# A K=32 matmul padded to all 128 rows, and the filler matmuls of an attention loop gathered ahead of the readout

## The chip, the cores and the metric

The kernel runs on one core of one Trainium2 chip. The metric is device time in microseconds (us) of one execution; the median of three runs is compared. Engines are called PE (TensorE), DVE (VectorE), ACT (ScalarE) and POOL (GpSimd); PEld is PE's loading of weights, which the trace lists apart from the matmuls. "Weights" of a matmul is its stationary operand, whatever tensor that is.

## The reference, cut to what matters

A two-layer decoder trunk over 256 tokens of width 1024: a gated DeltaNet layer, then a sparse-attention layer with three branches (compressed, selection, window). The change lies in the second layer. With 256 tokens every selected block and the whole window are visible, so the selection and window branches are both causal attention over 256 keys; the compressed branch attends over 15 block summaries.

```
q = rope((x @ w_in)[:, :1024])                      # 16 heads of 64, 4 key groups
z = (x @ w_in)[:, 1024:4096]                        # 3 branches x 16 heads x 64
gates = sigmoid((x @ w_in)[:, 4096:])
k_cmp, v_cmp = compress_blocks(...)                 # 15 rows per key group
o_cmp = masked_softmax(q @ k_cmp.T) @ v_cmp
o_sel, o_win = causal softmax attention over k_sel/v_sel, k_win/v_win
o = sum over the 3 branches of gates * o_branch * silu(z_branch)
x = layer_norm(sqrt(2) * x + o @ w_out)
```

## The kernel before

All of the stage runs in one hand-written order: an engine executes its instructions in the order in which the Python code issues them. Tokens are two tiles of 128 rows (t = 0, 1). A **unit** is one or two heads of one tile: for t = 0 two heads (h, h+1), for t = 1 one head. The string UNITS sets the order of the 24 units: (0,0), (0,2), (1,0), (0,4), (1,1), (0,6), (1,2), ... "Round i" below is pass i of the main loop, which starts unit i and finishes unit i-1. For a unit:

- `scores` (L1327): four PE matmuls into a bank `s` (two such banks).
- `maxima` (L1336 to L1343): DVE adds the mask and takes row maxima.
- `exps` (L1356 to L1361): ACT writes exponentials `pt` and, for the compressed branch, `Pc`.
- `transposes` (L1369, L1371): PE turns `pt` into bank `ptp`, and Pc into 32 rows of the `s` bank: two heads x 16 compressed positions.
- `probs` (L1376, L1380): ACT copies them to `PT` and `PcT` (32 rows x 128).
- `readout` (L1395, L1398, L1401): PE multiplies PT with the values `vtok` (65 columns), and PcT with `vbd`, the compressed values of two heads laid out block-diagonally (32 rows x 130 columns), into the one bank `op`. An f32 matmul is two PE instructions. For t = 1 a readout needs two heads; where these are neighbours in the order, it is done in halves, and only the second half has L1401.
- `total` (L1409 to L1413): DVE divides, gates and sums `op` into `zz`, issued by `defer(1, ...)` at the next `step()`.

The other work of the loop is the projection z (`bz`): 48 **parts**, each two weight chunks of 128x512, six matmuls of 512 columns in bank `pbz` (`tm_part`, L233 to L235, a product split into three by high and low halves). `fill(n)` issues n parts. FA[i] and FB[i] say how many a round issues ahead of `exps` and behind the readout. Weights come by DMA into `raw_bz`, ACT casts the high half (`hi_bz`, L181), POOL subtracts for the low half (`lo_bz`, L185); eight pairs of buffers hold them, and `presplit` issues up to one chunk more a round. When a tile's four parts are done, ACT and DVE make z's gate of them (`th` L1227, `zz` L1228). From round 18 on `merges` is not empty and the parts are those of the output projection (`pbo`, `pbl`); t = 1 heads are merged by `tp_b` (L1427).

Of the kernel before, what the change touches and what calls it, by code (L numbers as in the profile page):

```python
# [9 lines left out]
F32 = mybir.dt.float32  # L10
# [7 lines left out]
P = 128  # L18
# [20 lines left out]
FA = "3113111011210212044211123"  # L39
FB = "0211121311122110212111000"  # L40

PRE, TAIL = 4, 2
NEG = -1e30

NSEL = 9
# [3 lines left out]
def make_consts():  # L49
# [8 lines left out]
    c = np.zeros((P, NCON_B), np.float32)  # L58
    cm = np.where(f <= p, np.float32(0), np.float32(NEG))
    n = np.arange(16)[None, :]  # L60
    for off, t in ((C_CM0, p), (C_CM1, p + P)):
        c[:, off:off + P] = cm
        c[:, off + P:off + 2 * P] = cm
        c[:, off + 256:off + 272] = np.where((n < 15) & (16 * n + 31 <= t), np.float32(0), np.float32(NEG))
    c[:, C_ROW:C_ROW + 1] = p >= 31
# [28 lines left out]
def trunk(ctx: ExitStack, tc: tile.TileContext, I: dict, out: bass.AP):  # L94
    nc = tc.nc
    V, S, G, PE = nc.vector, nc.scalar, nc.gpsimd, nc.tensor
# [7 lines left out]
    def defer(n, f):  # L104
        late.append([n, f])

    def step():
        for e in late:
            e[0] -= 1
        due = [e for e in late if e[0] <= 0]  # L110
        late[:] = [e for e in late if e[0] > 0]
        for _, f in due:
            f()
# [15 lines left out]
    wk = ph.enter_context(tc.tile_pool(name="wk", bufs=3))  # L129
# [35 lines left out]
    def split_to(n):  # L165
        while state["s"] < min(n, len(order)):
            lower()
            load_to(state["s"] + (NRAW))
            k = order[state["s"]]
            state["s"] += 1  # L170
            if k[0] == "w1":
                continue
            r = raws[k]
            h = ring.tile([P, 1024], F32R, tag="whi", name=f"hi_{k[0]}_{k[1]}", bufs=NSPL)
            l = ring.tile([P, 1024], F32R, tag="wlo", name=f"lo_{k[0]}_{k[1]}", bufs=NSPL)
            if k == order[1]:

                S.copy(h[:, 0:512], r[:, 0:512])
                V.tensor_copy(h[:, 512:1024], r[:, 512:1024])
            else:  # L180
                S.copy(h, r)  # L181
            e = V if state["s"] <= NVEC + 1 else G

            def f(l=l, r=r, h=h):
                e.tensor_tensor(l, r, h.bitcast(F32), op=ALU.subtract)  # L185

            if e is G:
                f()
            else:
                lows.append(f)  # L190
            splits[k] = (h, l)
# [4 lines left out]
    def lower():  # L196
        while lows:
            lows.pop(0)()
# [42 lines left out]
    def presplit():  # L241
        oldest = next(i for i, n in enumerate(uses) if n)
        split_to(min(state["top"] + PRE, oldest + NSPL, state["s"] + 1))
        lower()

    def fill(n, low=True):
        for _ in range(n):
            step()
            if fills:
                fills.pop(0)()  # L250
            if low:
                lower()
# [174 lines left out]
    def decay_diff(q):  # L427
# [6 lines left out]
        def causal(e):  # L434

            G.affine_select(e, e, pattern=[[0, 4], [1, P]], base=0, channel_multiplier=-1,
                            compare_op=ALU.is_ge, fill=NEG)

# [567 lines left out]
    def pool(name, bufs, **kw):  # L1006
        return ph.enter_context(tc.tile_pool(name=name, bufs=bufs, reuse_waits="tile", **kw))
# [5 lines left out]
    wk = pool("wkb", 2)  # L1013
# [8 lines left out]
    def tbank(name):  # L1022
        return pt_.tile([P, 512], F32, tag="t", name=name)
# [77 lines left out]
    G.memset(hpS, 0.0)  # L1101
    hid = wk.tile([P, 2, 4, 16], F32, name="hid", bufs=1)
    G.memset(hid, 0.0)
    vbd = wk.tile([32, 4, 2, 65], F32, name="vbd", bufs=1)
    bd = cb[0:32, C_BD:C_BD + 2]
    G.tensor_copy(vbd[:, :, :, 64], bd[:, None, :].to_broadcast([32, 4, 2]))
    fill(2)
    k_post()
    fill(4)
# [76 lines left out]
    def compressed_v():  # L1186

        vcp = tbank("vcp")
        for g_ in range(4):
            PE.matmul(vcp[0:32, g_ * 64:(g_ + 1) * 64], hr[:, g_].rearrange("p a b -> p (a b)"), w2[:, 256:320],  # L1190
                      start=True, stop=True)

        def place():
            for g_ in range(4):
                V.tensor_tensor(vbd[:, g_, :, 0:64], vcp[0:32, None, g_ * 64:(g_ + 1) * 64].to_broadcast([32, 2, 64]),
                                bd[:, :, None].to_broadcast([32, 2, 64]), op=ALU.mult)

        defer(1, place)
# [115 lines left out]
    units = [order0.pop(0) if k == "0" else order1.pop(0) for k in UNITS]  # L1314
    S_, PT_, PTT, PC, PCT, MX, TP = {}, {}, {}, {}, {}, {}, {}
    cnt = {"n": 0}

    def scores(u):
        t, h = u
        sp = S_[u] = sbank(f"s{t}{h}")  # L1320
        for j in range(2):
            hh = h + j if t == 0 else h
            lq = qT[hh // 8][:, hh % 8, t * P:(t + 1) * P]
            n = 272 if t == 0 or j == 0 else 256
            c0 = 272 if t == 1 and j == 1 else 0
            for i, kk in enumerate((kh, kl)):
                PE.matmul(sp[:, j, 0:n], lq, kk[:, hh // 4, c0:c0 + n], start=i == 0, stop=i == 1)  # L1327
# [17 lines left out]
    def exps(u):  # L1345
        t, h = u
        sp, mx = S_[u], MX[u]
        s4 = sp[:, :, 0:256].rearrange("p j (b k) -> p j b k", b=2)
        pt = PT_[u] = wk.tile([P, 2, 2, P], F32, tag="hl", name=f"pt{t}{h}", bufs=3)
        if t == 0 or h % 2 == 0:  # L1350
            PC[t, h] = wk.tile([P, 2, 16], F32, tag="Pc", name=f"Pc{t}{h}", bufs=4)
        Pc = PC[t, h - h % 2]
        if t == 0:
            for j in range(2):
                for b in range(2):
                    S.activation(pt[:, j, b, :], s4[:, j, b, :], AF.Exp, bias=mx[:, 2 * j + b:2 * j + b + 1])  # L1356
                S.activation(Pc[:, j, :], sp[:, j, 256:272], AF.Exp, bias=mx[:, 4 + j:5 + j])
        else:
            for b in range(2):
                S.activation(pt[:, :, b, :], s4[:, :, b, :], AF.Exp, bias=mx[:, b:b + 1])  # L1360
            S.activation(Pc[:, h % 2, :], sp[:, 0, 256:272], AF.Exp, bias=mx[:, 4:5])  # L1361

    def transposes(u):
        t, h = u
        pt = PT_[u]
        tp = TP[u] = tbank(f"ptp{t}{h}")
        for j in range(2):
            for b in range(2):
                PE.transpose(tp[:, (2 * j + b) * P:(2 * j + b + 1) * P], pt[:, j, b, :], ident)  # L1369
        if t == 0 or h % 2:  # L1370
            PE.transpose(S_[u][0:32, 1, 272:400], PC[t, h - h % 2 * t].rearrange("p a b -> p (a b)"), ident)  # L1371

    def probs(u):
        t, h = u
        PT = PTT[u] = wk.tile([P, 2, 2, P], F32, tag="ra", name=f"PT{t}{h}", bufs=6)
        S.copy(PT.rearrange("p a b c -> p (a b c)"), TP[u])  # L1376
        if t == 0 or h % 2:
            h -= h % 2 * t
            PCT[t, h] = wk.tile([32, P], F32, tag="PcT", name=f"PcT{t}{h}", bufs=2)
            S.copy(PCT[t, h], S_[u][0:32, 1, 272:400])  # L1380

    OP, summed = {}, set()

# [82 lines left out]
    merges, ready = [], []  # L1466
    cnt["t0"] = 0

    def advance():
        if merges:  # L1470
            merges.pop(0)()

    def merge0(q):
        merge(0, 4 * q, 4, tbank)
        if q:
            add_bo(0, [(c, part) for c in range(2) for part in range(4)])

    def merge1(g_):
        need_z(1, 3072)
        merge(1, 2 * g_, 2, tbank)  # L1480
        add_bo(1, [(0, g_)])
        if g_ == 3:
            add_bo(1, [(1, g_)])

    n = len(units)
    for i in range(n + 1):
        if i < n:
            scores(units[i])
        first = i < n and units[i][0] == 0 and not merges
        if first:  # L1490

            maxima(units[i])
        if i:
            probs(units[i - 1])
        step()
        if i < n and not first:
            maxima(units[i])
        fill(int(FA[i]))
        advance()
        presplit()  # L1500
        if i < n:
            exps(units[i])
        if i:
            t, h = units[i - 1]
            if t == 0:
                readout(t, h)
                if h == 14:
                    cnt["t0"] = 1
                    merges += [lambda: merge0(0), lambda: merge0(1)] + ready
            else:  # L1510

                if (units[i - 2] if h % 2 else units[i]) == (1, h ^ 1):
                    readout(t, h - h % 2, h % 2)
                elif h % 2:
                    readout(t, h - 1)
                if h % 4 == 3:
                    (merges if cnt["t0"] else ready).append(lambda g_=h // 4: merge1(g_))
        fill(int(FB[i]))
        if i < n:
            transposes(units[i])  # L1520
    while len(merges) > 1:
# [78 lines left out]
```

## Time and profile before

| | |
|---|---|
| median of 3 runs | 393.53 us (392.84 to 394.13) |
| the profiled execution | 393.95 us, its span 392.2 us |
| PE busy | 379.5 us of the span, 97% |
| DVE, ACT, POOL busy | 223.5, 220.4, 246.2 us |
| mean granted TensorE clock | 0.995 |

The busy time of PE overlaps itself (matmuls are pipelined and their ends are modelled), so the cost of PE work is read below from one start to the next start, not from durations.

### The profile page before, as it was taken

The numbers are of one execution on the slowest core, as the hardware profiler recorded it, in microseconds if no ns is written. First come the engines' busy times: TensorE is split into PE (matmuls) and PEld (weight loads), VectorE is DVE, ScalarE is ACT, GpSimd is POOL, SyncE is SP. The second block draws the span as 40 slices with busy tenths as digits, with TensorE's granted clock in tenths as the row PEclk, the third lists the DMA queues.
The fourth block names the chain that finished last, engine by engine and source line by source line (L and its number), as shares of the span: only waits on it lengthen the run. The fifth ranks groups of instructions, "written<-read, shape, count | busy, mean of one in ns | idle before, by whom it ended". The sixth has DMA issues, their size and how long they took to land.

```text
span 392.2 us, 7553 instructions
## 1 busy us (share of the span) xinstructions
PE 379.5 (97%) x2870; PEld 334.8 (85%) x2870; DVE 223.5 (57%) x591; ACT 220.4 (56%) x433; POOL 246.2 (63%) x154
## 2 busy tenths in 40 slices
PE   8999999999999999999999999999999999999991
PEld 6899999999979987877998788888888888878891
DVE  2868776678633455454541655645656465676726
ACT  4688766656654462625563649566474647456410
POOL 5699999747454846894754988193544637209051
PEclk9999999999999999999999999999999999999998
DMA  7876678754334315573636764343515243301011
GB/s 223 323 223 206 223 220 293 200 135 164 110 113 146 119 45 171 175 242 119 214 109 213 274 222 152 107 150 119 162 43 174 65 151 109 107 3 53 3 53 53
DMA packets 23476, 58.68 MB, mean 150 GB/s; under 512 B 6672, under 2 KB 9232, under 8 KB 23312
## 3 DMA queue, kind: packets, MB, share of 16 engines
q1 hardware_dynamic: 23232, 58.13, 44.7%
q8 instruction: 22, 0.36, 0.4%
q14 instruction: 14, 0.11, 0.1%
q10 hardware_dynamic: 144, 0.07, 0.1%
q0 software_dynamic: 64, 0.01, 0.0%
HBM read 55.96 MB, written 2.23 MB: 148 GB/s over the span
## 4 chain that ended last, share of the span: by engine, by line
PE 42%; DVE 4%; ACT 3%; DMA 2%; POOL 2%; issue 1%; POOLq 0%; DVEq 0%; SPq 0%; ACTq 0%
PE pbz L233 6%; PE pbz L234 6%; PE pbz L235 6%; PE op L1398 4%; PE s L1327 3%; PE ptp L1369 3%; DMA raw_bz<-in_bz 2%; PE op L1401 2%; PE op L1395 1%; ACT hi_bq L181 1%; POOL lo_bq L185 1%; PE pskv L235 1%; PE pbo L233 1%; PE pskv L233 1%; PE pskv L234 1%; PE qtp L1214 1%
## 5 line engine op out<-in xcount | busy, mean ns | idle before, releaser
L185 POOL TENSOR_TENSOR lo_bz<-raw_bz,hi_bz 128x1024 fp32r<-128x1024 f32 x24 | 56.8, 2390 | 39.1 <-ACT hi_bz L181 21.5
L185 POOL TENSOR_TENSOR lo_wqkv<-raw_wqkv,hi_wqkv 128x1024 fp32r<-128x1024 f32 x22 | 52.4, 2399 | 6.8 <-ACT hi_wqkv L181 4.7
L233 PE MATMUL pbz<-hi_bz,x1h 128*128 128x512 f32 x96 | 38.9, 405 | 0.0
L234 PE MATMUL pbz<-hi_bz,x1l 128*128 128x512 f32 x96 | 37.7, 393 | 0.0
L235 PE MATMUL pbz<-lo_bz,x1h 128*128 128x512 f32 x96 | 37.6, 392 | 0.0
L185 POOL TENSOR_TENSOR lo_bo<-raw_bo,hi_bo 128x1024 fp32r<-128x1024 f32 x8 | 18.8, 2384 | 22.8 <-ACT hi_bo L181 17.7
L185 POOL TENSOR_TENSOR lo_skv<-raw_skv,hi_skv 128x1024 fp32r<-128x1024 f32 x12 | 28.4, 2401 | 5.0 <-PE pskv L235 5.0
L185 POOL TENSOR_TENSOR lo_wz<-raw_wz,hi_wz 128x1024 fp32r<-128x1024 f32 x8 | 19.4, 2438 | 16.0 <-ACT hi_wz L181 15.9
L1376 ACT COPY PT<-ptp 128x512 f32<-128x512 f32 x24 | 14.1, 587 | 24.4 <-PE ptp L1369 24.4
L181 ACT CAST hi_bz<-raw_bz 128x1024 fp32r<-128x1024 f32 x24 | 25.3, 1053 | 2.9 <-DMA raw_bz<-in_bz 1.6
L185 POOL TENSOR_TENSOR lo_wo<-raw_wo,hi_wo 128x1024 fp32r<-128x1024 f32 x8 | 18.9, 2387 | 11.8 <-ACT hi_wo L181 11.8
L185 POOL TENSOR_TENSOR lo_bq<-raw_bq,hi_bq 128x1024 fp32r<-128x1024 f32 x8 | 19.1, 2394 | 11.6 <-ACT hi_bq L181 11.6
L181 ACT CAST hi_wqkv<-raw_wqkv 128x1024 fp32r<-128x1024 f32 x22 | 22.7, 1043 | 1.2 <-DMA raw_wqkv<-in_wqkv 1.2
L235 PEld LDWEIGHTS pbz<-lo_bz,x1h 128*128 128x128 f32 x96 | 18.0, 188 | 4.1
L233 PEld LDWEIGHTS pbz<-hi_bz,x1h 128*128 128x128 f32 x96 | 18.0, 188 | 4.1
L234 PEld LDWEIGHTS pbz<-hi_bz,x1l 128*128 128x128 f32 x96 | 18.0, 188 | 2.8
L1360 ACT ACTIVATE pt<-s,mx 128x256 f32<-128x256 f32 x32 | 13.4, 472 | 10.9 <-DVE mx L1343 8.7
L215 PE MATMUL pk<-xh,hi_wqkv 128*128 128x256 f32 x64 | 18.7, 292 | 0.0
L215 PE MATMUL pq<-xh,hi_wqkv 128*128 128x256 f32 x64 | 18.5, 289 | 0.0
L217 PE MATMUL pk<-xh,lo_wqkv 128*128 128x256 f32 x64 | 18.1, 283 | 0.0
L217 PE MATMUL pq<-xh,lo_wqkv 128*128 128x256 f32 x64 | 18.1, 283 | 0.0
L216 PE MATMUL pq<-xl,hi_wqkv 128*128 128x256 f32 x64 | 18.1, 283 | 0.0
(360 smaller groups left out, 1257.3 us busy)
## 6 DMA issues: line engine op xcount, KB each, us to landing
raw_bz<-in_bz SPq DMA_DIRECT2D x24, 512.0 KB, 3.3
raw_wqkv<-in_wqkv SPq DMA_DIRECT2D x23, 512.0 KB, 4.5
raw_skv<-in_skv SPq DMA_DIRECT2D x12, 512.0 KB, 3.3
raw_wz<-in_wz SPq DMA_DIRECT2D x8, 512.0 KB, 3.3
raw_wo<-in_wo SPq DMA_DIRECT2D x8, 512.0 KB, 3.4
raw_bq<-in_bq SPq DMA_DIRECT2D x8, 512.0 KB, 3.7
raw_bo<-in_bo SPq DMA_DIRECT2D x8, 512.0 KB, 3.3
raw_w<-in_w SPq DMA_DIRECT2D x4, 512.0 KB, 3.3
```

Source lines behind the costliest of these rows:

```text
L181: S.copy(h, r)
L185: e.tensor_tensor(l, r, h.bitcast(F32), op=ALU.subtract)
L215: PE.matmul(ps[:, 0:T], wh[:, kt, :], ah[:, kt, :], start=kt == 0, stop=False)
L216: PE.matmul(ps[:, 0:T], wh[:, kt, :], al_[:, kt, :], start=False, stop=False)
L217: PE.matmul(ps[:, 0:T], wl[:, kt, :], ah[:, kt, :], start=False, stop=kt == 7)
L233: PE.matmul(ps, ah[:, kt, tt], wh[:, k4, cols], start=kt == 0, stop=False)
L234: PE.matmul(ps, al_[:, kt, tt], wh[:, k4, cols], start=False, stop=False)
L235: PE.matmul(ps, ah[:, kt, tt], wl[:, k4, cols], start=False, stop=kt == 7)
L1327: PE.matmul(sp[:, j, 0:n], lq, kk[:, hh // 4, c0:c0 + n], start=i == 0, stop=i == 1)
L1360: S.activation(pt[:, :, b, :], s4[:, :, b, :], AF.Exp, bias=mx[:, b:b + 1])
L1376: S.copy(PT.rearrange("p a b c -> p (a b c)"), TP[u])
L1398: PE.matmul(o3[:, r, 1 + b, :], PT[:, j, b, :], vt_[:, b, j, g_, :], start=j == 0, stop=j == 1)
```

## The change

Two edits. First, `vbd` and the two `PcT` buffers have 128 rows, whose rows 32 to 127 are set to zero once by POOL; L1401 then takes 128 rows instead of 32. ACT still copies only 32 rows. Second, while `merges` is empty (rounds 0 to 17), a round issues one part, then `exps`, then the rest of FA[i]+FB[i], and then `presplit`, the readout and the transposes, with no part between those two. The rest is as it was.

```diff
-    vbd = wk.tile([32, 4, 2, 65], F32, name="vbd", bufs=1)
+    vbd = wk.tile([P, 4, 2, 65], F32, name="vbd", bufs=1)
+    G.memset(vbd, 0.0)
+    pct = [wk.tile([P, P], F32, name=f"PcT{i}", bufs=1) for i in range(2)]
+    for c_ in pct:
+        G.memset(c_, 0.0)
...
-            PCT[t, h] = wk.tile([32, P], F32, tag="PcT", name=f"PcT{t}{h}", bufs=2)
-            S.copy(PCT[t, h], S_[u][0:32, 1, 272:400])
+            PCT[t, h] = pct[len(PCT) % 2]
+            S.copy(PCT[t, h][0:32, :], S_[u][0:32, 1, 272:400])
...
-        fill(int(FA[i]))
-        advance()
-        presplit()
-        if i < n:
+        fa, fb = int(FA[i]), int(FB[i])
+        if not merges and i < LAST:
+            fa, fb = fa + fb, 0
+            fill(1)
             exps(units[i])
+            fill(fa - 1)
+            presplit()
+        else:
+            fill(fa)
+            advance()
+            presplit()
+            if i < n:
+                exps(units[i])
...
-        fill(int(FB[i]))
+        fill(fb)
```

PE in round 8, before: the readout of unit (0,6), bank `op06`, with a part on each side (line numbers are those of the kernel that is listed).

```order
L235 MATMUL pbz30_3441<-lo_bz_13_3393,x1h_2043 128x512
L1395 MATMUL op06_3485<-vtok_2284,PT06_3465 128x65 x4
L1401 MATMUL op06_3485<-vbd_2386,PcT06_3467 128x2x65
L233 MATMUL pbz30_3441<-hi_bz_14_3404,x1h_2043 128x512
L234 MATMUL pbz30_3441<-hi_bz_14_3404,x1l_2044 128x512
L235 MATMUL pbz30_3441<-lo_bz_14_3405,x1h_2043 128x512
L233 MATMUL pbz30_3441<-hi_bz_14_3404,x1h_2043 128x512
L234 MATMUL pbz30_3441<-hi_bz_14_3404,x1l_2044 128x512
L235 MATMUL pbz30_3441<-lo_bz_14_3405,x1h_2043 128x512
L1369 MATMUL ptp12_3503<-ident_112,pt12_3480 128x128 x4
```

The same place of the changed kernel, whose lines are numbered six higher here (L1407 is L1401 of before, L1375 is L1369) and one higher in the projection.

```order
L234 MATMUL pbz30_3461<-hi_bz_13_3401,x1h_2043 128x512
L235 MATMUL pbz30_3461<-hi_bz_13_3401,x1l_2044 128x512
L236 MATMUL pbz30_3461<-lo_bz_13_3402,x1h_2043 128x512
L1401 MATMUL op06_3485<-vtok_2284,PT06_3445 128x65 x4
L1407 MATMUL op06_3485<-vbd_2386,PcT0_2388 128x2x65
L1375 MATMUL ptp12_3492<-ident_112,pt12_3474 128x128 x4
L1333 MATMUL s08_3497<-kh_2282,qT1_2696 128x272
```

Both parts now stand ahead of the readout, and the transpositions of unit (1,2) follow it at once.

ACT in rounds 2 and 3, before: the casts of the weight chunks 8, 9 and 10 of `bz` around the exponentials of unit (1,0).

```order
L1376 COPY PT02_3192<-ptp02_3181 128x512
L1380 COPY PcT02_3194<-s02_3126 32x128
L181 CAST hi_bz_8_3203<-raw_bz_8_3000 128x1024
L181 CAST hi_bz_9_3215<-raw_bz_9_3021 128x1024
L1360 ACTIVATE pt10_3219<-s10_3187,mx10_3196 128x2x128 x2
L1361 ACTIVATE Pc10_3220<-s10_3187,mx10_3196 128x16
L1376 COPY PT10_3256<-ptp10_3242 128x512
L181 CAST hi_bz_10_3260<-raw_bz_10_3042 128x1024
```

And in the changed kernel:

```order
L182 CAST hi_bz_8_3175<-raw_bz_8_3005 128x1024
L1382 COPY PT02_3197<-ptp02_3186 128x512
L1386 COPY PcT1_2389<-s02_3131 32x128
L1366 ACTIVATE pt10_3216<-s10_3192,mx10_3205 128x2x128 x2
L1367 ACTIVATE Pc10_3217<-s10_3192,mx10_3205 128x16
L182 CAST hi_bz_9_3223<-raw_bz_9_3026 128x1024
L182 CAST hi_bz_10_3235<-raw_bz_10_3047 128x1024
L1382 COPY PT10_3260<-ptp10_3246 128x512
```

Chunk 9 moved from ahead of the exponentials to behind them; chunk 8 moved forward. Both kernels use chunks 9 and 10 first in round 3.

## Rows read from the trace of the kernel before

**Rows 1.** Windows, the main loop while z is projected: busy us of each engine (instructions), clock.
```profile
241.00:343.00 102.00, 102.00 (x585) 87.06 (x584) 58.48 (x138) 61.58 (x144) 52.86 (x23) 1.00 0.37 123
```
**Rows 2.** Timeline of PE, rounds 8 and 9: start us, duration us, engine, line, operation, output<-inputs.
```profile
278.43 0.60 PE L1369 MATMUL ptp<-ident,pt 128*128 128x128 f32 x4
...
279.46 0.40 PE L233 MATMUL pbz<-hi_bz,x1h 128*128 128x512 f32 x1
...
280.83 1.00 PE L1395 MATMUL op<-vtok,PT 128*128 128x65 f32 x8
281.76 0.48 PE L1401 MATMUL op<-vbd,PcT 32*128 32x130 f32 x2
282.18 0.50 PE L233 MATMUL pbz<-hi_bz,x1h 128*128 128x512 f32 x1
...
283.69 0.60 PE L1369 MATMUL ptp<-ident,pt 128*128 128x128 f32 x4
284.05 0.37 PE L1327 MATMUL s<-kh,qT 128*128 128x272 f32 x1
```
**Rows 3.** Timeline of PE's weight loads at the same readout.
```profile
281.50 0.19 PEld L1395 LDWEIGHTS op<-vtok,PT 128*128 128x128 f32 x1
...
281.76 0.29 PEld L1401 LDWEIGHTS op<-vbd,PcT 32*128 32x128 f32 x2
```
**Rows 4.** Timeline of PE, rounds 21 and 22: half readouts without and with L1401.
```profile
359.61 1.00 PE L1398 MATMUL op<-vtok,PT 128*128 128x65 f32 x8
360.42 0.48 PE L233 MATMUL pbo<-hi_bo,x1h 128*128 128x512 f32 x1
...
365.45 0.48 PE L1401 MATMUL op<-vbd,PcT 32*128 32x130 f32 x2
365.87 0.66 PE L1369 MATMUL ptp<-ident,pt 128*128 128x128 f32 x4
366.28 0.37 PE L1327 MATMUL s<-kh,qT 128*128 128x272 f32 x1
```
**Rows 5.** Timeline of weight loads in the first layer: 128-row loads, then four of 32.
```profile
13.62 0.19 PEld L365 LDWEIGHTS pv<-xh,hi_wqkv 128*128 128x128 f32 x1
13.74 0.19 PEld L365 LDWEIGHTS pv<-xl,hi_wqkv 128*128 128x128 f32 x1
14.06 0.52 PEld L368 LDWEIGHTS gps<-pair,ba 32*128 32x128 f32 x4
```
**Rows 6.** Timeline, all engines: maxima, exponentials, a cast, a total, a low half.
```profile
265.48 0.43 DVE L1340 TENSOR_TENSOR s<-s,cb 128x256 f32<-128x256 f32 x1 [3.80 <-PE s L1327]
...
267.05 0.84 ACT L1360 ACTIVATE pt<-s,mx 128x256 f32<-128x256 f32 x2 [1.44 <-DVE mx L1343]
...
267.77 0.27 ACT L1361 ACTIVATE Pc<-s,mx 128x16 f32<-128x16 f32 x1
...
268.41 1.06 ACT L181 CAST hi_bz<-raw_bz 128x1024 fp32r<-128x1024 f32 x1
...
269.46 0.20 DVE L1409 RECIPROCAL op<-op 128x6 f32<-128x6 f32 x1 [0.20 <-PE op L1401]
...
269.55 2.39 POOL L185 TENSOR_TENSOR lo_bz<-raw_bz,hi_bz 128x1024 fp32r<-128x1024 f32 x1 [4.72 <-ACT hi_bz L181]
...
271.09 0.56 DVE L1413 TENSOR_REDUCE zz<-op 128x128 f32<-128x384 f32 x1
```
**Rows 7.** The chain that ended last, where the last parts of z end.
```profile
340.74 0.24 PE pbz L235
...
344.51 2.00 PE op L1398 x16
...
349.21 0.88 PE op L1398 x6
```
**Rows 8.** Timeline of POOL: idle us ahead of it and its releaser in brackets.
```profile
183.17 9.47 POOL L185 TENSOR_TENSOR lo_skv<-raw_skv,hi_skv 128x1024 fp32r<-128x1024 f32 x4 [4.98 <-PE pskv L235]
```
**Rows 9.** Groups by line of POOL, shapes apart: count, busy us, mean ns.
```profile
L695 POOL MEMSET Xr<- 128x512 f32 x2 | 1.0, 520 | 0.0
```

More of the change, by code (lines that the diff above doesn't have):

```diff
@@ L42 @@
 PRE, TAIL = 4, 2
+LAST = 20
 NEG = -1e30
@@ L1103, in trunk @@
     G.memset(hid, 0.0)
-    vbd = wk.tile([32, 4, 2, 65], F32, name="vbd", bufs=1)
+    vbd = wk.tile([P, 4, 2, 65], F32, name="vbd", bufs=1)
[3 more added lines that the diff above has]
+        G.memset(c_, 0.0)
     bd = cb[0:32, C_BD:C_BD + 2]
-    G.tensor_copy(vbd[:, :, :, 64], bd[:, None, :].to_broadcast([32, 4, 2]))
+    G.tensor_copy(vbd[0:32, :, :, 64], bd[:, None, :].to_broadcast([32, 4, 2]))
     fill(2)
@@ L1194, in place @@
             for g_ in range(4):
-                V.tensor_tensor(vbd[:, g_, :, 0:64], vcp[0:32, None, g_ * 64:(g_ + 1) * 64].to_broadcast([32, 2, 64]),
+                V.tensor_tensor(vbd[0:32, g_, :, 0:64], vcp[0:32, None, g_ * 64:(g_ + 1) * 64].to_broadcast([32, 2, 64]),
                                 bd[:, :, None].to_broadcast([32, 2, 64]), op=ALU.mult)
```

## The prediction

> **What bounds the kernel now.** I read the windows first, since one share for the whole program mixes its stages. From 241 to 343 us, rounds 0 to 17, PE is busy in all 102.00 us, at a granted clock of 1.00 (the 2.4 GHz level), while DVE, ACT and POOL are busy a little over half of it [rows 1]. So a us less of PE work there is a us less of time, as long as the others keep up. Next the timeline of PE, read from start to start, for what each kind of work costs; there the trace is odd at one place. Six matmuls of a part take 1.37 us when they follow the scores (279.46 to 280.83) but 1.51 when they follow L1401 (282.18 to 283.69), and L1401, two instructions with 130 columns, takes 0.42, against 0.10 for one of the 65-column matmuls ahead of it [rows 2, 4]. Last, the chain, for the places where PE does wait: from the last part of z at 340.74 to the readout at 344.51 it runs through ACT and DVE [rows 7].
>
> **Edit one: L1401 with 128 rows.** Eight full-row matmuls take 0.81 when something full-row follows (359.61 to 360.42), but 0.93 when L1401 follows (280.83 to 281.76) [rows 2, 4]. The load of L1401's weights starts 0.26 after the previous load (281.50 to 281.76), where its own second load starts 0.10 behind the first (0.29 for the two, 0.19 for one); that is, PE finishes the running matmul first [rows 3]. Four loads of 32 rows in the first layer show the same: 0.32 from load to load, where 0.12 is usual [rows 5]. Behind L1401 the same seems to be paid again: 1.51 instead of 1.37 for a part, 0.41 (365.87 to 366.28) instead of 0.36 (283.69 to 284.05) for four transpositions [rows 2, 4]. I take these waits as a cost of changing between 32 and 128 rows.
>
> With 128 rows L1401 becomes two more steps of the readout's kind. No row shows 130 columns with full rows. Its lower bound is the 0.10 a step of rows 4; the upper is today's 0.42 for the pair. It is nearest to the first, because the loads have as many columns as the readout's; as 130 columns stream twice as long as 65, I take 0.106 a step, 1.06 for eight and two.
>
> The Trainium skill, page "TensorEngine Tiling (Array Packing)", section "Tiling Modes", says that changing the tiling mode drains TensorE; by it the waits go with the change of mode, as in my sum. Against the edit speaks the page "TensorE: Matmul & The Clock Gate", section "Part 3: Packing small matmuls": a weight load overlaps running matmuls only where the row groups differ. By that, a full-row L1401 could not load ahead at all and nothing would be won (rival B). This trace disagrees: eight loads with the same 128 rows keep a pace of 0.10 a step.
>
> The zeros cost POOL one 128x520 and two 128x128 memsets, 776 columns in all: at the 0.52 us that 512 columns take, 0.8 [rows 9]. They stand in the 4.98 us in which POOL waits for PE ahead of 183.17, so nothing moves [rows 8]; uncovered they would be 0.8 us, once.
>
> **Edit two: the parts in one lot.** The number of parts is the same. In ten rounds (1, 2, 4, 5, 6, 8, 9, 11, 12, 14) a part stood behind the readout; now transpositions do. Per such round, before: 0.93 + 0.42 + 1.51 = 2.86. After: 1.37 + 1.06 = 2.43, with the same transpositions behind. That is 0.43, ten times, 4.3 us. Sixteen-step readouts differ by the same. Round 15 had no part behind its readout: 0.93 + 0.42 + 0.41 = 1.76 becomes 1.06 + 0.36 = 1.42, 0.34 less. So the last part of z ends 4.64 us earlier.
>
> Rounds 17 and 18 lie beside the wait: 340.74 to 344.51 is ACT and DVE work behind the last part, unchanged, so round 17's saving is lost there. From 344.51 to 349.21 there is one readout with L1401, then its total: 0.33 less (0.12 of entry, 0.21 of the pair). Round 22 is as round 15, 0.34. Rounds 20 and 24 keep a part behind the readout; its 1.51 I leave as it is (whether it pays for L1401's rows or for following the readout, no row here tells), so each saves 0.93 + 0.42 - 1.06 = 0.29. In all 4.64 + 0.33 + 0.34 + 0.58 = 5.9 us.
>
> **What gets late.** The exponentials are issued one part into a round, and casts that stood ahead of them may now queue behind them on ACT. The tightest place is rounds 2 and 3. Count from the end of the readout in round 1. `total` starts 0.2 later (L1401's modelled end is 0.06 behind the next start in rows 2, and 0.14 of wait is gone); it takes 2.19 (269.46 to 271.65), and unit (1,0)'s maxima stand behind it on DVE: ready at 2.4 + 1.57 = 3.95 (265.48 to 267.05), `pt` at 4.8, Pc at 4.95 [rows 6]. PE meanwhile needs 1.03 for transpositions and scores (278.43 to 279.46), 2 x 1.37 and 1.06: it comes to the next transpositions at 4.83 [rows 2]. Covered, by 0.03, and in round 6 likewise. In the rounds 9, 12 and 15, with sixteen-step readouts, the margin is 0.9. Behind Pc wait the casts of chunks 9 and 10, 1.06 each: 6.0 and 7.1; their low halves, 2.39 each on POOL: 8.4 and 10.8 [rows 6]. PE starts round 3 at 4.83 + 0.95 = 5.8, and the fourth part, which reads low half 10 in its third matmul, needs it at 5.8 + 3 x 1.37 + 0.46 = 10.35. PE waits 0.45. For the other chunks the same count leaves 0.8 or more, since they are cast a round ahead of use, or for a third part. The one bank `op` is free in time in round 5: maxima (taken as 1.57 like those above) and the `total` of the round before (2.19), 0.2 behind the scores, end at 4.0; three parts take 4.1.
>
> Sum: 5.9 - 0.45 = 5.45 us. The profiled execution took 393.95 (span 392.2), so 388.5; the median of the runs is 0.42 lower, so 388.1.
>
> **Rivals.**
> - A, the forecast: 388.1. With the wait in round 3 absent 387.6, and with 0.10 a step (0.06 less in each of 16 readouts) 386.7; with 0.11 a step (0.04 more in each) and another wait of 0.45, 389.2.
> - B, the 32 rows are not what PE waits for but the 130 columns, or the weights that ACT copied, or that a load cannot run ahead of a matmul on the same rows (the rule quoted above). Then 0.93 + 0.42 stays. Only ten parts behind a readout become cheaper: 1.51 - 1.37 - 0.05 = 0.09 each, 0.9 in all, less 0.45: 393.1. For it: no row has 130 columns with full rows. Against: rows 5, where the columns and the writer are others and the wait is the same.
> - C, the waits go but ACT and DVE fall behind more often: the margins near zero in rounds 2 and 6 fail by one cast each that stands ahead of the exponentials on ACT (1.06), and chunk 10 comes 0.5 later still. Some 2.6 us (2 x 1.06 + 0.5) are given back: 390.7. For it: these two margins, and that of the bank `op` in round 5. Against: all other rounds have 0.8 and more.
> - D, slower: low halves come late for every chunk. Sixteen chunks are cast inside the loop, now mostly behind the exponentials, which themselves wait for DVE; each then needs 1.06 + 2.39 before PE can use it. If each of the sixteen cost what I count for one, 0.45, that is 7.2 us, more than the 5.9 won: 393.5 + 1.3 = 394.8. It decides from 0.37 a chunk on, and passes the bound of a measurable loss at 0.45. Against: POOL is busy for 52.86 of 102 us, so it can catch up, and the count above finds one tight chunk.
> - E, faster still: 386.5 or less, if the parts behind the scores too gain from the quieter DVE.
>
> **Chances.** A 0.67, B 0.07, C 0.18, D 0.05, E 0.03. What a measurement here can tell is about 0.3%, 1.2 us: B counts as no change, D as slower, or, where it costs less, as no change. Faster 0.87, same 0.08, slower 0.05. The range takes in A with its lower bound and most of C: 386.7 to 390.4.
>
> **What would show it.** Right: the load of L1401's weights 0.10 to 0.11 behind the previous one, the next matmul about 0.11 behind L1401's second, no part above 1.40; the readout with L1401 near 1.06 where it took 1.35. The first part of z starting as before, the last one 4 us or more earlier. Wrong by B: 0.42 at L1401 again. Wrong by C: gaps in PE ahead of the transpositions in rounds 2, 5, 6, released by ACT `pt`. Wrong by D: gaps ahead of the third matmul of a part, released by POOL `lo_bz`, in more rounds than round 3.

## The result, and the profile after

The changed kernel takes 391.94 us (median of 7 runs, 390.91 to 393.49) against 393.7 for the kernel before (7 runs, 392.84 to 394.88): ratio 0.9948, 95% interval 0.9923 to 0.9973. It is faster by some 2 us; forecast were 5.45 us, 388.1, and a range of 386.7 to 390.4 that does not hold the result. The profiled execution took 390.99 us, its span is 389.3. Of the 2.9 us between the two spans 0.86 lie ahead of the loop (first scores at 240.38 instead of 241.24); over this kernel, the one before and the seven of the experiments that start lies between 239.7 and 241.8 with no order in it, so it is left out below.

The window of the main loop, with the columns of [rows 1]:

```profile
241.00:343.00 102.00, 99.74 (x591) 86.18 (x589) 59.49 (x143) 61.47 (x145) 52.22 (x22) 1.00 0.37 121
```

PE, which was busy in all 102.00 us, now has 2.26 us without a matmul; the clock is the same. So work did go, and waits came in. The timeline of PE in round 8:

```profile
288.42 0.40 PE L234 MATMUL pbz<-hi_bz,x1h 128*128 128x512 f32 x1
...
291.15 1.00 PE L1401 MATMUL op<-vtok,PT 128*128 128x65 f32 x8
291.99 0.44 PE L1407 MATMUL op<-vbd,PcT 128*128 128x130 f32 x2
292.27 0.60 PE L1375 MATMUL ptp<-ident,pt 128*128 128x128 f32 x4
292.70 0.27 PE L1377 MATMUL s<-ident,Pc 128*32 128x128 f32 x1
```

And its weight loads at the end of that readout, as in [rows 3]:

```profile
291.71 0.30 PEld L1401 LDWEIGHTS op<-vtok,PT 128*128 128x128 f32 x2
291.93 0.30 PEld L1407 LDWEIGHTS op<-vbd,PcT 128*128 128x128 f32 x2
```

[rows 2] and the two listings of PE under the change are not of this round. They are labelled rounds 8 and 9, and round 8, but the transpositions in them are of unit (1,2), which round 6 starts. The costs are those of round 8 all the same: there the kernel before takes 0.93 for the eight matmuls, 0.42 for the pair and 1.51 for the part (291.13, 292.06, 292.48 and 293.99 in its trace).

Here the change does what it says. The eight matmuls take 0.84 (291.15 to 291.99) where they took 0.93, the pair (now L1407) 0.28 where it took 0.42; its loads start 0.22 behind the two before them, which is 0.11 a load. Nothing waits in this round: two parts take 2.73 (288.42 to 291.15), and the scores follow the transpositions at once. The round is 4.88 us long from scores to scores, 0.38 less than before (5.26).

Two rounds earlier it looks different. The timeline of all engines in round 6, where the readout of round 5 has just ended:

```profile
275.33 0.60 PE L1375 MATMUL ptp<-ident,pt 128*128 128x128 f32 x4
...
275.97 0.59 ACT L1382 COPY PT<-ptp 128x512 f32<-128x512 f32 x1 [1.58 <-PE ptp L1375]
...
276.61 0.59 ACT L1233 ACTIVATE th<-pbz 128x512 f32<-128x512 f32 x1
...
277.22 0.69 DVE L1234 SCALAR_TENSOR_TENSOR zz<-th,pbz 128x512 f32<-128x512 f32 x1 [4.20 <-ACT th L1233]
277.83 0.20 DVE L1415 RECIPROCAL op<-op 128x6 f32<-128x6 f32 x1
...
279.46 0.56 DVE L1419 TENSOR_REDUCE zz<-op 128x128 f32<-128x384 f32 x1
279.94 0.42 DVE L1346 TENSOR_TENSOR s<-s,cb 128x256 f32<-128x256 f32 x1
280.17 1.08 PE L1401 MATMUL op<-vtok,PT 128*128 128x65 f32 x8 [0.91 <-DVE zz L1419]
...
281.48 0.84 ACT L1366 ACTIVATE pt<-s,mx 128x256 f32<-128x256 f32 x2 [3.35 <-DVE mx L1349]
282.00 0.91 PE L1375 MATMUL ptp<-ident,pt 128*128 128x128 f32 x4 [0.49 <-ACT pt L1366]
```

Read it by the brackets, from the end. PE waits for ACT's exponentials, these for DVE's maxima (3.35 of idle), and the readout waits for the end of `total`, which must empty the one bank `op`. `total` starts at 277.83, 2.5 us after the end of the readout that it belongs to (taken as the start of the transpositions, 275.33). What held it is the row above: DVE was idle for 4.20 us with `zz` at the head of its queue, and `zz` waited for `th`. ACT could have done `th` early, since the z tile was complete before the readout, but in ACT's order it stands behind the copy PT, which had to wait for the transpositions of 275.33. In the old loop it does not: every part begins with a `step()`, so a part behind the readout issues what was deferred ahead of the next PT. The round takes 6.88 us instead of 5.15.

The wait that was forecast for round 3 is there too: the third matmul of the fourth part, on PE, and POOL's low halves.

```profile
261.56 0.39 PE L235 MATMUL pbz<-hi_bz,x1l 128*128 128x512 f32 x1
262.07 0.50 PE L236 MATMUL pbz<-lo_bz,x1h 128*128 128x512 f32 x1
```
```profile
257.24 7.27 POOL L186 TENSOR_TENSOR lo_bz<-raw_bz,hi_bz 128x1024 fp32r<-128x1024 f32 x3 [3.47 <-ACT hi_bz L182]
```

0.51 from start to start instead of 0.23: POOL, which had been idle for 3.47 us until the cast came, does three low halves on end, and the second is done at about 262.0. With the slower start of the matmul behind it (0.33 later instead of 0.23) the round loses about 0.4: it takes 6.95 us, against 6.53 with edit one alone.

The memsets of edit one lie where they were expected, in POOL's idle time ahead of [rows 8]:

```profile
178.07 0.53 POOL L1107 MEMSET vbd<- 128x520 f32 x1
178.55 0.35 POOL L1110 MEMSET PcT<- 128x128 f32 x2
...
183.22 2.40 POOL L186 TENSOR_TENSOR lo_skv<-raw_skv,hi_skv 128x1024 fp32r<-128x1024 f32 x1 [4.18 <-PE pskv L236]
```

Behind round 17 the readout of round 22, which [rows 4] has for the kernel before, gains less than it should:

```profile
362.76 0.44 PE L1407 MATMUL op<-vbd,PcT 128*128 128x130 f32 x2
363.09 0.74 PE L1375 MATMUL ptp<-ident,pt 128*128 128x128 f32 x4
363.58 0.37 PE L1333 MATMUL s<-kh,qT 128*128 128x272 f32 x1
```

The pair takes 0.33 instead of 0.42, but the four transpositions 0.49 instead of 0.41.

### The profile page after: what moved, and what is told of

The parts are those of the page before. It is cut to its first block, busy times and chain, and to the rows that moved or that the text cites. A ratio compares the mean times of both kernels' runs of the same rounds, so it can differ in the third digit from the quotient of the medians.

```text
span 389.3 us, 7548 instructions
## 1 busy us (share of the span) xinstructions
PE 375.2 (96%) x2870; PEld 332.9 (86%) x2870; DVE 222.5 (57%) x591; ACT 219.9 (56%) x433; POOL 247.4 (64%) x157
## 4 chain that ended last, share of the span: by engine, by line
PE 86%; DVE 4%; POOL 3%; issue 2%; DMA 2%; ACT 1%; SPq 0%; POOLq 0%; DVEq 0%; ACTq 0%
PE pbz L236 5%; PE pbz L234 5%; PE pbz L235 5%; PE op L1404 4%; PE ptp L1375 3%; PE s L1333 3%; PE pwz L234 2%; PE pbq L234 2%; PE pk L218 2%; PE pk L216 2%; PE pwo L236 2%; PE pq L216 2%; PE pq L217 2%; PE pk L217 2%; PE pq L218 2%
## 5 line engine op out<-in xcount | busy, mean ns | idle before, releaser
L234 PE MATMUL pbz<-hi_bz,x1h 128*128 128x512 f32 x96 | 37.8, 393 | 0.0
L1234 DVE SCALAR_TENSOR_TENSOR zz<-th,pbz 128x512 f32<-128x512 f32 x12 | 8.2, 686 | 18.3 <-ACT th L1233 18.3
```

The source lines that it names most:

```text
L234: PE.matmul(ps, ah[:, kt, tt], wh[:, k4, cols], start=kt == 0, stop=False)
```

## The experiments

Each was timed in five rounds beside the kernel before, on the same chip, except the two with fewer rows, which ran once each, for their trace.

**Edit one alone, edit two alone, and a fix of round 6.** The first kernel has the 128 rows and the old loop; the second the new loop and 32 rows. The third is the changed kernel with one line:

```diff
             fill(fa - 1)
+            step()
             presplit()
```

Edit one alone: 

> The kernel before with edit one alone (128 rows in L1401; the parts stay on both sides of the readout). Theory 1 (the 32-row matmul's two waits cost what the trace of before shows, and the gathering of the parts is what gave most of the gain back): per readout the entry falls from 0.93 to 0.84, the pair from 0.42 to about 0.31 where a part follows and 0.28 where transpositions do, and the part behind it from 1.51 to 1.48, so 0.35 in ten rounds and about 0.28 in six: 4.5 to 5 us, ratio to before 0.987 to 0.989, and no wait of PE ahead of the readout of round 6. Rival (the loop is held by ACT and DVE as soon as PE is faster, whatever the order): 2 us as in the changed kernel, ratio 0.995, with new waits of PE in other rounds.

Measured: 388.8 us against 393.44, ratio 0.9886 (0.9864 to 0.9908). The timeline of PE in round 8, with lines numbered as in the changed kernel:

```profile
289.89 1.00 PE L1401 MATMUL op<-vtok,PT 128*128 128x65 f32 x8
290.73 0.44 PE L1407 MATMUL op<-vbd,PcT 128*128 128x130 f32 x2
290.93 0.48 PE L234 MATMUL pbz<-hi_bz,x1h 128*128 128x512 f32 x1
...
292.40 0.60 PE L1375 MATMUL ptp<-ident,pt 128*128 128x128 f32 x4
```

The readout takes 0.84, the pair 0.20 where 0.31 was expected ahead of a part, the part behind it 1.47. So edit one by itself is worth 4.5 us, more than twice what the change as a whole gave. The rival falls: with a faster PE and the old loop there is no wait in round 6 (4.82 us).

Edit two alone: 

> The kernel before with edit two alone (parts in one lot, L1401 keeps 32 rows). Theory 1: the lot loses some 2.5 us in the rounds 3 and 6 and wins about 0.1 in each of ten rounds: slower by 1 to 2 us, ratio 1.002 to 1.005, with PE waiting about 1 us ahead of the readout of round 6 and again ahead of its transpositions. Rival (the lot is harmless, the smaller gain comes from L1401 alone): faster by 0.5 to 1 us, ratio 0.998, and no wait in round 6.

Measured: 395.42 us, ratio 1.0059 (1.0039 to 1.008), a loss of 2.3 us, a little more than the most that was expected. Round 6 in its timeline (L1396 is the readout, L1410 the start of `total`):

```profile
279.05 0.59 ACT L1228 ACTIVATE th<-pbz 128x512 f32<-128x512 f32 x1
...
279.67 0.69 DVE L1229 SCALAR_TENSOR_TENSOR zz<-th,pbz 128x512 f32<-128x512 f32 x1 [4.42 <-ACT th L1228]
280.28 0.20 DVE L1410 RECIPROCAL op<-op 128x6 f32<-128x6 f32 x1
...
282.62 1.08 PE L1396 MATMUL op<-vtok,PT 128*128 128x65 f32 x8 [0.91 <-DVE zz L1414]
```

It is the chain of the changed kernel, with the old slow L1401. By the ratios the two edits add up within the noise: -4.5 and +2.3 against -2. By the traces, counted from the first scores to the end, they do not quite: -4.4 and +1.5 against -2.1 (last column of the table below). Most of the difference is a gain that either edit brings alone: in rounds 8 and 9 the lot saves 0.09 and 0.11 us with 32 rows, but 0.06 and 0.03 with 128.

The fix: 

> The changed kernel with one more step() behind the lot's last part, so that the gate of z (th on ACT, zz on DVE) of a tile that ends in the lot is issued ahead of the next round's copies PT, and not between them and the total. Theory 1 (in round 6 zz waits for th, th stands behind PT and PcT on ACT, and the total and the maxima stand behind zz on DVE): the waits of PE in round 6 (1.1 ahead of the readout, 0.9 around the transpositions) go, 1.5 to 2 us less than the changed kernel, ratio to before about 0.990. Rival (the total itself is too long to fit ahead of the maxima and the one bank op): PE still waits about 1 us in round 6, and the time is that of the changed kernel, ratio 0.995.

Measured: 388.96 us, ratio 0.9886 (0.9863 to 0.9909), some 2.4 us better than the changed kernel by the ratios. In its round 6:

```profile
275.06 0.63 ACT L1233 ACTIVATE th<-pbz 128x512 f32<-128x512 f32 x1
275.73 0.69 DVE L1234 SCALAR_TENSOR_TENSOR zz<-th,pbz 128x512 f32<-128x512 f32 x1 [1.89 <-ACT th L1233]
...
276.34 0.20 DVE L1415 RECIPROCAL op<-op 128x6 f32<-128x6 f32 x1
...
276.71 0.59 ACT L1382 COPY PT<-ptp 128x512 f32<-128x512 f32 x1 [1.01 <-PE ptp L1375]
...
279.85 1.00 PE L1401 MATMUL op<-vtok,PT 128*128 128x65 f32 x8
```

`th` now stands ahead of PT, `total` starts 0.26 us behind the readout's end (276.08) instead of 2.5, and the readout of round 6 follows its parts without a wait. The round takes 4.78.

**Does DVE's order alone do it?** The step() moves two things, `th` on ACT and `zz` on DVE. This kernel is the changed one with `zz` of that one tile a step later; ACT's order stays as it was.

```diff
-                defer(1, lambda: done(c, t, pst[t]))
+                defer(2 if (w, c, t) == ("bz", 1, 1) else 1, lambda: done(c, t, pst[t]))
```

> The changed kernel in which one instruction of DVE moves: the zz of the tile that ends in round 5 (pbz11) is issued one step later, so on DVE it stands behind unit (1,2)'s maxima instead of ahead of the total of round 5's readout; its th stays where it was on ACT, behind PT and PcT. Theory 1a (PE's wait in round 6 comes from the place of zz in DVE's queue): the readout of round 6 follows its parts at once (gap 0.23 instead of 1.30), the wait ahead of the transpositions shrinks to 0.3 or less, about 1.5 to 2 us less than the changed kernel, ratio to before 0.990. Rival 1b (th itself, late on ACT, delays the exponentials or the gate that the total reads): the gap in round 6 stays near 1 us and the ratio near 0.995.

Measured: 388.95 us, ratio 0.9886 (0.9868 to 0.9904). Its round 6:

```profile
274.89 0.20 DVE L1415 RECIPROCAL op<-op 128x6 f32<-128x6 f32 x1 [2.43 <-PE op L1407]
...
275.97 0.58 ACT L1233 ACTIVATE th<-pbz 128x512 f32<-128x512 f32 x1
...
277.00 0.42 DVE L1346 TENSOR_TENSOR s<-s,cb 128x256 f32<-128x256 f32 x1
...
278.37 0.68 DVE L1234 SCALAR_TENSOR_TENSOR zz<-th,pbz 128x512 f32<-128x512 f32 x1
278.49 1.00 PE L1401 MATMUL op<-vtok,PT 128*128 128x65 f32 x8
278.55 0.84 ACT L1366 ACTIVATE pt<-s,mx 128x256 f32<-128x256 f32 x2 [1.06 <-DVE mx L1349]
...
279.61 0.60 PE L1375 MATMUL ptp<-ident,pt 128*128 128x128 f32 x4
```

`th` is as late as before, behind PT, and does no harm. `total` starts 0.20 behind the readout's end (274.69), as the prediction had counted, and all of the 2.1 us of round 6 is gone (4.80 us). One instruction of 0.69 us at the wrong place of DVE's queue, where it waited for `th`, cost as much as the whole change gained.

**The casts behind the exponentials.** The changed kernel with the step() of above, and presplit moved:

```diff
             fill(1)
+            presplit()
             exps(units[i])
             fill(fa - 1)
-            presplit()
+            step()
```

> The changed kernel with step() behind the lot, as before, and with presplit ahead of the exponentials, so that a chunk's cast does not stand behind them. Theory 2 (the 0.4 us that PE waits for the low half in round 3 comes from casts behind the exponentials): that wait goes, in round 4 too, 0.5 us less than with step() alone: ratio to before 0.987 to 0.988, the fastest version. Rival (casts ahead of the exponentials delay these, and PE then waits ahead of the transpositions): the same time as with step() alone, or up to 0.5 us more, with a wait ahead of the transpositions in some round.

Measured: 389.33 us, ratio 0.99 (0.9881 to 0.992), not to be told from the step() alone. It was expected to be the fastest version, by 0.5 us, and is not. Round 3 lost its wait (6.55 instead of 6.95), but the trace of PE has the same wait one round later:

```profile
263.67 0.39 PE L235 MATMUL pbz<-hi_bz,x1l 128*128 128x512 f32 x1
264.26 0.50 PE L236 MATMUL pbz<-lo_bz,x1h 128*128 128x512 f32 x1 [0.20 <-POOL lo_bz L186]
```

Round 4 takes 5.37 where it took 4.98 with the step() alone. The next chunk, 11, is cast behind the exponentials of round 3 in this order as in the other, and POOL then takes its 2.4 us. The theory has the right engine, and the remedy only moved the wait.

**How many rows?** Both kernels are the changed one with fewer rows of the same buffers handed to L1407, so the sums are the same.

```diff
-        PE.matmul(o3[:, :, 0, :], PCT[t, h], vbd[:, g_, :, :], start=True, stop=True)
+        PE.matmul(o3[:, :, 0, :], PCT[t, h][0:64, :], vbd[0:64, g_, :, :], start=True, stop=True)
```

64 rows: 

> The changed kernel with 64 of the 128 rows handed to L1401 (the other rows are zero in any case). Theory 1 (PE waits where weights of another number of rows than 128 follow or precede): the load of L1401's weights again starts about 0.26 behind the previous one and what follows again starts about 0.2 behind its second matmul, the pair 0.42. Rival (only 32 rows are special, or the waits came from the narrow tile that ACT wrote): load 0.11 behind the previous one and the pair 0.28, as with 128 rows.

96 rows (0:96 in the same line): 

> The changed kernel with 96 of the 128 rows handed to L1401. The earlier look at 64 rows brought both waits back. Theory 1 in its narrow form (any other number of rows than 128): pair 0.42 and load 0.26 behind the previous one again. Rival (96 rows load like 128: a matmul with 96-row weights earlier in this program, L1297, follows 128-row ones at the usual pace): pair 0.28, load 0.11 behind.

The timeline of PE with 64 rows, and then with 96:

```profile
293.18 1.00 PE L1401 MATMUL op<-vtok,PT 128*128 128x65 f32 x8
294.10 0.49 PE L1407 MATMUL op<-vbd,PcT 64*128 64x130 f32 x2
294.52 0.66 PE L1375 MATMUL ptp<-ident,pt 128*128 128x128 f32 x4
```
```profile
290.90 1.00 PE L1401 MATMUL op<-vtok,PT 128*128 128x65 f32 x8
291.74 0.44 PE L1407 MATMUL op<-vbd,PcT 96*128 96x130 f32 x2
292.02 0.60 PE L1375 MATMUL ptp<-ident,pt 128*128 128x128 f32 x4
```

With 64 rows 0.92 and 0.42, the cost of 32 to 0.01 us; with 96 rows 0.84 and 0.28, that of 128. Since the operands, the writer of PcT and the 130 columns are the same in both, it is the number of rows that PE waits for, and the narrow form of the theory (anything but 128) is wrong. The Trainium skill, page "TensorEngine Tiling (Array Packing)", section "Tiling Modes", says that changing the tiling mode drains TensorE. These runs agree with it for 32 and 64 rows, in that a wait appears there. But the same section of the Trainium skill also lists 128 rows by 32 columns as a configuration. L1377, which has such weights, shows no wait: the scores start 0.03 to 0.04 behind it in every trace here.

The whole kernel took 395.82 us with 64 rows and 390.75 with 96, one run each. The run with 64 rows shows a second cost of the wait in round 6, in its windows with the columns of [rows 1]:

```profile
278.00:282.90 4.90, 3.62 (x20) 2.58 (x19) 3.60 (x10) 1.56 (x4) 2.77 (x2) 1.00 0.62 201
282.90:286.30 3.40, 3.40 (x12) 3.01 (x13) 1.64 (x5) 0.64 (x3) 0.00 (x0) 0.50 0.28 107
```

Behind a stretch in which PE worked for only 3.62 of 4.90 us, the granted clock is 0.50, the 1.2 GHz level, for 3.4 us, and round 7 takes 6.58 us instead of 5.18. The changed kernel has the same wait, and the clock in its trace does not fall there, so the waits themselves do not settle when it does. Of the ten runs of edit two alone, which has the wait too, three show a mean granted clock of 0.989 and took 396.87 to 397.37 us; the other seven, at 0.993 and more, took 394.63 to 396.05. Whether the clock fell at the same place in those three was not traced.

Lengths of rounds from the traces, first scores matmul to first scores matmul, us; then the sum of the rounds 0 to 17, and the time from the first scores to the last matmul of z and to the end of the kernel.

| kernel | round 3 | 4 | 6 | 8 | 9 | 0 to 17 | last of z | end |
|---|---|---|---|---|---|---|---|---|
| before | 6.52 | 6.62 | 5.15 | 5.26 | 6.05 | 101.55 | 99.34 | 151.0 |
| changed | 6.95 | 5.02 | 6.88 | 4.88 | 5.68 | 99.89 | 98.09 | 148.9 |
| edit one alone | 6.53 | 6.27 | 4.82 | 4.94 | 5.71 | 98.06 | 95.83 | 146.6 |
| edit two alone | 6.57 | 5.65 | 6.88 | 5.17 | 5.94 | 102.85 | 100.75 | 152.5 |
| with step() | 6.94 | 4.98 | 4.78 | 4.87 | 5.68 | 97.53 | 95.72 | 146.4 |
| zz later | 6.97 | 4.96 | 4.80 | 4.87 | 5.68 | 97.65 | 95.85 | 146.6 |
| step() and presplit | 6.55 | 5.37 | 4.81 | 4.88 | 5.68 | 97.58 | 95.78 | 146.5 |

(Round 4 has three parts where the loop is the old one, since the readout asks for one more of z, and two in the lot; the third then comes in round 17. So the sum of the rounds 0 to 17 ends at another place of z's work in the two loops, and the column "last of z" is the one to compare.)

## Why the prediction was wrong

- **The cause of the odd cost at L1401: right**, shown by 128, 64 and 32 rows, with one bound: 96 rows pay nothing. Edit one alone gave 4.5 us.
- **The size of the readout: too small.** "I take 0.106 a step, 1.06 for eight and two": it measured 0.84 and 0.28, unrounded 1.114. The step from the pair's first matmul to its second is 0.166, not 0.106. Over the eleven readouts ahead of the last part of z that is some 0.6 us, over all sixteen 0.8.
- **"`total` starts 0.2 later ... Covered, by 0.03, and in round 6 likewise": the step that failed.** In round 2 it held. In round 6, the round that [rows 2] shows, the count left out what stands ahead of `total` in DVE's queue. With the last part of the lot a z tile ends; its gate is deferred to the next `step()`, which in the lot comes behind the next round's PT copy. So `zz` waited for `th`, `th` for PT, and `total`, the maxima, the readout and the exponentials for `zz`: 6.88 - 4.80 = 2.1 us. The rows of ACT and DVE that it counted with [rows 6] are those of round 4 of the kernel before; for round 6 it counted nothing of its own. Rival C named round 6, but for a cast on ACT, and at half the price.
- **The wait in round 3: right** in place, cause and size (about 0.4 for 0.45), though a remedy moved it instead of removing it.
- **"Ten rounds ... 0.43": right for the two edits together but for the size above, wrong in how it is shared out.** Rounds 8 and 9 became 0.38 and 0.37 shorter. The 0.14 by which a part is slower behind L1401 was booked to the gathering of the parts. Edit one alone brings 0.04 of it (1.47), and lets the part's first matmul start 0.20 behind the pair's first, where the transpositions start 0.28 behind it. In round 9 the lot then saves 0.03 (5.71 to 5.68), in round 8 0.06, not 0.14. Without its wait in round 6 the changed kernel comes to 0.9886, the same as edit one alone: over the whole kernel next to nothing is left of edit two (0.1 us up to the last of z).
- **The wait behind z: right.** From the last matmul of z to the readout of round 18 it is 3.9 us in both kernels.
- **Behind it: too much.** Rounds 18 (from its readout on), 20 and 22 were to give 0.33, 0.29 and 0.34 us, and gave 0.16, 0.32 and 0.09. In rounds 18 and 22 a part of the pair's saving became a wait in the transpositions (0.49 instead of 0.41 in both). In round 22 the second transposition starts at 363.28, just behind the end of the exponentials at 363.23; that it waits for them fits, but was not tried.

The last part of z was to come 4.64 - 0.45 = 4.2 us earlier, counted from the first scores, and came 1.25 earlier (98.09 instead of 99.34). Of the 2.9 that are missing 2.1 are round 6 and 0.6 the size of the readout; the rest, some 0.3, was not traced to a place. With the size of the readout put right the forecast would be 388.1 + 0.8 = 388.9, and the kernel without the wait in round 6 took 388.95. That they agree so closely is luck: the terms behind the wait were too large as well, and the interval of that kernel's ratio is 0.7 us to either side.

Rival B fell with edit one alone. D fell with round 6, where one gate cost the time and not sixteen chunks.

## What to carry to other kernels

A matmul with few rows in its weights among full ones (here 32 or 64) can cost more than its own time: look at the starts of weight loads on both sides of it, and pad with zero rows if PE is what ends last. When work is reordered around a stage, write down the queue of every in-order engine ahead of the instruction that matters, round by round: what is deferred "to the next step" moves with it, and a short instruction that waits at the head of a queue holds all that stands behind. Time two edits of one change apart; here one gave 4.5 us and the other took half of it back, and no profile of the two together says so as plainly.

## What the runs showed of the hardware

- Weights of 32 or 64 rows between 128-row ones cost the same 0.09 on entry and, ahead of transpositions, 0.14 in the pair; 96 rows cost as little as 128. I had expected every other number to pay.
- Full-row loads ran ahead of full-row matmuls in every trace, at 0.11 a load: L1407's first load starts at 291.93, beside the last matmul of L1401, which starts at 291.88. The Trainium skill, page "TensorE: Matmul & The Clock Gate", section "Part 3: Packing small matmuls", has a sentence by which loads overlap running matmuls only where the row groups differ. Taken by itself that is not what these traces show; the section also names a background weight buffer as a second way, and no run here tells whether that is the one at work.
- The pair with 130 columns takes 0.166 from its first matmul to its second and 0.11 from the second to the next f32 matmul; ahead of a part, whose matmuls are fp32r and have 512 columns, the latter is 0.03, and the part's second matmul then comes 0.32 behind its first instead of 0.23. So what a readout costs depends on the matmul that follows; whether by its type or by its columns no run tells apart.
